# One order of the six matmuls of a tile in all plain products of a hybrid convolution encoder step

## The chip, the cores and the metric

The kernel runs as one program on one core of a Trainium2 chip. The metric is the device time of one execution in microseconds, taken as the median of three runs. The profile is of one more execution, whose own time is a little longer.

## What is computed

One layer of a streaming encoder for 576 tokens (512 of a new stream, 64 of a running one) with 1024 features: a SwiGLU feed-forward layer (FFN), a mixer with two gated convolution branches, a second FFN, and a final norm. Cut to the matrix products:

```python
def swiglu_ffn(x, w_gate_up, w_down):
    gate, up = jnp.split(x @ w_gate_up, 2, axis=-1)
    return (jax.nn.silu(gate) * up) @ w_down

def encoder_layer(...):
    x = x + 0.5 * swiglu_ffn(rms_norm(x, ffn1_norm), ffn1_w_gate_up, ffn1_w_down)
    h = rms_norm(x, mix_norm)
    p = h @ w_in          # 7 blocks of 1024: B, C, V of branch A; U (two) of branch B; two gates
    ...
    y_a = (a_b * a_conv) @ w_a_out
    ...
    y_b = b_act @ w_b_out
    merged = jax.nn.sigmoid(gate_a) * y_a + jax.nn.sigmoid(gate_b) * y_b
    x = x + merged @ w_out
    x = x + 0.5 * swiglu_ffn(rms_norm(x, ffn2_norm), ffn2_w_gate_up, ffn2_w_down)
```

Everything is float32.

## The kernel before

Features lie on the 128 partitions and the 576 tokens along the free axis, in two halves of 288 (`HALVES`, called half 0 and half 1 here). A product makes 128 output features for all tokens. It has one PSUM tile of two banks, one bank for each half, and adds up its input features in tiles of 128 (8 tiles for 1024 inputs, 5 or 6 for a group of hidden features of the FFN).

Each float32 operand is split into a high part, rounded to the format that TensorE takes at full rate (`float32r`), and the low rest. A tile of a product is then six matmuls of 128x128 weights against 128x288 activations: high weights by high activations, high weights by low activations, low weights by high activations, each for half 0 and half 1. In the code these are numbered `n` = 0, 1, 2 and `s` = 0, 1. Below they are written H0 and H1 (both high), L0 and L1 (low activations), W0 and W1 (low weights). All six add into the bank of their half, so any order gives the same sum up to rounding. Each matmul has its own weight load, also where two in a row use the same weights.

The order of the six is what the change is about. Before, there are six of them:

- `mm`, the ordinary one: H0 H1 L0 L1 W0 W1. It is used by the plain gate and up products of the FFNs, by the down projections ("d") and by `o`, the product with `w_out`.
- `THREES`, H0 L0 W0 H1 L1 W1: blocks 4 and 3 of `w_in` (branch B), 16 products.
- `MIRROR`, H0 L0 L1 H1 W1 W0: blocks 1, 2 and 0 (branch A), 24 products.
- `ALONE`, all eight tiles of half 0 (H0 L0 W0 each), then all eight of half 1: block 5 and `ya`, 16 products.
- `SIXES`, as ALONE but two tiles at a time: block 6, 8 products.
- `TWOS`, H0 L0 H1 L1 W0 W1: `yb`, 8 products.

In the order of time the program has: the start and three plain pairs of gate and up products; the other pairs of the first FFN, which are not plain (`pair` makes a gate and an up tile of seven half-size products, each with its own loop over H, L, W, untouched by the change); after each of four groups of hidden features, eight down projections; the mixer in the order of the list above from THREES to TWOS, then `o`; the second FFN with one plain pair; and a tail in which the last six down projections are done for 304 tokens and then for 272 (`LATE_SPANS`), with one span at a time.

Weights come by DMA from the SP queue; ScalarE (ACT) makes the high part, GpSimd (POOL) adds the low part up by a DMA. `ws.get` and `chunks` hand them over and issue the work for later ones. A product with a pattern or an order takes all its weights first and then issues its matmuls (`chunks`); an ordinary one takes them unit by unit (four tiles) in between. VectorE (DVE) reads the sums out of PSUM, and has the 31-tap convolution of branch B to do beside it: `fill` hands it pieces of that work by an estimate of how far it is behind TensorE, and the block of statements around `advance` makes the two sums of its layer norm on TensorE.

The instructions of each engine stand in the order in which the program is written.

Of the kernel before, what the change touches and what calls it, by code (L numbers as in the profile page):

```python
# [15 lines left out]
KT = D // P  # L16
# [6 lines left out]
H = T // 2  # L23
# [29 lines left out]
IN_TURN = (0, 4, 1, 5, 2, 6, 3, 7)  # L53


THREES = [(0, n, s) for s in range(2) for n in range(3)]
MIRROR = [(0, 0, 0), (0, 1, 0), (0, 1, 1), (0, 0, 1), (0, 2, 1), (0, 2, 0)]
TWOS = [(0, 0, 0), (0, 1, 0), (0, 0, 1), (0, 1, 1), (0, 2, 0), (0, 2, 1)]
SIXES = [(k, n, s) for s in range(2) for k in range(2) for n in range(3)]
ALONE = [(k, n, s) for s in range(2) for k in range(KT) for n in range(3)]  # L60

RAWS = 6

# [44 lines left out]
def tile_encoder_step(  # L108
# [7 lines left out]
    pe, dve, sca, pool = (  # L116
        Ordered(tc, e, c)
        for e, c in (
            (nc.tensor, pe_cost), (nc.vector, dve_cost), (nc.scalar, None), (nc.gpsimd, None)
        )  # L120
    )
# [31 lines left out]
    def psum2():  # L153
        return mmps.tile([P, 2, 512], F32, tag="mm", name=nm("mm"))
# [13 lines left out]
    def half(ap, s):  # L168
        return ap[:, s * H : (s + 1) * H]
# [223 lines left out]
    def mm(ps, w, kk, xs, first, last, spans=HALVES):  # L393


        (whi, wlo), (xh, xl) = w, xs
        for n, (a, b) in enumerate(((whi, xh), (whi, xl), (wlo, xh))):
            for s, (i, e) in enumerate(spans):
                pe.matmul(
                    ps[:, s, : e - i], a[:, kk, :], b[:, i:e],  # L400
                    start=first and n == 0, stop=last and n == 2,
                )

    def chunks(name):

        got = []
        for n in plan[name]:
            w = ws.get(n)
            got += [(w, kk) for kk in range(ws.units[n][1])]
        return got  # L410
# [10 lines left out]
    def take():  # L421

        while behind:
            ready, then = behind.pop(0)
            dve.time = max(dve.time, ready)
            then()

    early = {}

    def patterned(ps, got, xs, order, pattern):  # L430

        tiles = 1 + max(k for k, _, _ in pattern)
        todo = [
            (order[at + k], n, s) for at in range(0, len(xs), tiles) for k, n, s in pattern
        ]
        ends = {s: i for i, (_, _, s) in enumerate(todo)}
        begun = set()
        for i, (k, n, s) in enumerate(todo):
            ((whi, wlo), kk), (xh, xl) = got[k], xs[k]
            a, b = ((whi, xh), (whi, xl), (wlo, xh))[n]  # L440
            pe.matmul(
                ps[:, s, :H], a[:, kk, :], half(b, s), start=s not in begun, stop=ends[s] == i
            )
            begun.add(s)

    def product(name, xs, then=None, order=None, got=None, pattern=None):

        if name in early:
            return early.pop(name)[:, :, :H]
        ps = psum2()  # L450
        if pattern:
            patterned(ps, chunks(name), xs, order or range(len(xs)), pattern)
        elif order or got:
            got = got or chunks(name)
            for n, k in enumerate(order or range(len(xs))):
                mm(ps, *got[k], xs[k], n == 0, n == len(xs) - 1)
        else:
            k = 0
            for n in plan[name]:
                w = ws.get(n)  # L460
                for kk in range(ws.units[n][1]):
                    mm(ps, w, kk, xs[k], k == 0, k == len(xs) - 1)
                    k += 1
        take()
        if then is None:
            dve.time = max(dve.time, pe.time)
            return ps[:, :, :H]
        fill()
        behind.append((pe.time, lambda: then(ps[:, :, :H])))
# [145 lines left out]
    xg = []  # L615
# [58 lines left out]
    for k in range(KT):  # L674
        if k == KT - 1:
            R1 = rstd(ss)
        for name in FIRST:
            w, kk = firstw[name][k]
            mm(first[name], w, kk, xg[k], k == 0, k == KT - 1)
    early.update(first)  # L680
    name = ("f1", "u", 1)
    ps = product(name, xg)
# [131 lines left out]
    ss, xg = nss, nxg  # L814
# [71 lines left out]
    def gate_b(j, raw):  # L886
        def then(ps):
            t = gates[j] = ttile()
            if raw:
                dve.tensor_tensor(halves(t), ps, halves(R), op=ALU.mult)  # L890
                sca.activation(t, t, AF.Sigmoid)
                dve.tensor_tensor(t, t, R, op=ALU.mult)
            else:
                sca.activation(halves(t), ps, AF.Sigmoid)
        return then

    def value_b(j):
        G = gtile()
        history(G, HB, j, R_HB)

        def then(ps):
            gate(ps, gates.pop(j), G, HB)
            keep_history(G, HB, LB, j, 0)
            taps_of(j, G)
        return then

    for j in range(KT):
        raw = j < RAW_J
        xs = xg if raw else xn
        product(("p", 4, j), xs, gate_b(j, raw), pattern=THREES)  # L910
        if R is None:
            R = rstd(ss)
        if raw:
            xn.extend(scaled(range(3 * j, min(KT, 3 * j + 3)), R))
        product(("p", 3, j), xs, value_b(j), pattern=THREES)
    xg = xn

    AB = []
# [34 lines left out]

    for j in range(KT):
        for b, of in ((1, c_of), (2, cv_of), (0, b_of)):
            product(("p", b, j), xg, of(j), pattern=MIRROR)

    M, SGB, BA = [], [], []

# [23 lines left out]
    def ga_of(j):  # L983
        def then(ps):
            t = gates[j] = ttile()
            sca.activation(halves(t), ps, AF.Sigmoid)
        return then

    def ya_of(j):
        def then(ps):  # L990
            m = atile() if j < 4 else wtile(n=T)
            dve.tensor_tensor(halves(m), ps, halves(gates.pop(j)), op=ALU.mult)
            M.append(m)
        return then
# [22 lines left out]
    for j in range(KT):  # L1017
        if j == 5:
            while len(C) < KT:
                work.pop(0)()  # L1020
        product(("p", 5, j), xg, ga_of(j), pattern=ALONE)
        advance()
        product(("ya", j), AB, ya_of(j), pattern=ALONE)
        advance()
    take()
    sca.dma_start(hist.rearrange("(j p) n -> p j n", p=P), hst)
# [6 lines left out]
    def gb_of(j):  # L1033
        def then(ps):
            while work and j >= 2 and len(BA) < j - 1:
                work.pop(0)()
            sg = wtile(n=T) if j < 2 else gtile(n=T)
            sca.activation(halves(sg), ps, AF.Sigmoid)
            SGB.append(sg)
        return then  # L1040

    for j in range(KT):
        product(("p", 6, j), xg, gb_of(j), pattern=SIXES)
    while work:
        work.pop(0)()
    take()

    MS = []
    for j in range(KT):
        ps = product(("yb", j), BA, pattern=TWOS)  # L1050
        dve.tensor_tensor(halves(SGB[j]), ps, halves(SGB[j]), op=ALU.mult)
        dve.tensor_tensor(M[j], M[j], SGB[j], op=ALU.add)
        MS.append(split(M[j]))

    ss = Sum()
    xg = [None] * KT
    forms = Forms(R_N2)
    for n, j in enumerate(IN_TURN):
        ps = product(("o", j), MS)
# [4 lines left out]
        p = n // 2  # L1064
# [116 lines left out]
```

## Time and profile before

| what | value |
|---|---|
| median of 3 runs | 1329.13 us (1328.92 to 1329.64) |
| the profiled execution | 1331.87 us |
| its span, first to last instruction | 1330.1 us |
| TensorE busy, share of the span | 1301.9 us, 98% |
| matmul instructions | 9746 |
| VectorE, ScalarE, GpSimd busy | 895.4, 776.7, 399.8 us |
| mean granted TensorE clock | 0.996 of full speed |

A matmul's busy time in the trace is about 295 ns, but matmuls are pipelined and their records overlap, so the busy time says only that TensorE always had one in flight. What counts is the distance from the start of one matmul to the start of the next. The timeline gives it: it merges matmuls with operands of the same names into one row with a count, and since the weights of a product lie by turns in buffers `u`, `g` and `act`, a row is half a product (12, 18 or 24 matmuls). The start of a row less the start of an earlier one, over the matmuls in between, is the mean distance, called the pitch here.

### The profile page before, as it was taken

To read this page: it belongs to the slowest core of one execution; us is meant where nothing else is said; L and a number is where in the kernel's file an instruction comes from. 1 tells how busy PE (TensorE), PEld (TensorE's weight loads), DVE (VectorE), ACT (ScalarE), POOL (GpSimd) and SP (SyncE) were. 2 spreads that over 40 slices of the span, in tenths; PEclk is the share of its full clock that TensorE was granted. 3 is DMA by queue.
4 is the path that set the end of the run, shared out by engine and by line. 5 is a ranking of instruction groups with operands and counts; after the bars stand their busy time and mean duration, and the time that the engine had idled before them with its cause. 6 is when DMAs were issued, how large, how long until landed. Compare 5 with 4: busy or idle time off the path is not lost.

```text
span 1330.1 us, 25704 instructions
## 1 busy us (share of the span) xinstructions
PE 1301.9 (98%) x9746; PEld 1296.1 (97%) x9746; DVE 895.4 (67%) x1468; ACT 776.7 (58%) x1369; POOL 399.8 (30%) x504
## 2 busy tenths in 40 slices
PE   8999999999999999999999999999899999999995
PEld 8999999999999999999999999999899999999995
DVE  6848758748845998888884160336767858837944
ACT  8655646645666655555545574466665656644673
POOL 4142332232233453332222322221242242231242
PEclk9999999999999999999999999999999999999998
DMA  9497786886798897787775977775697696796692
GB/s 243 103 185 154 161 178 154 175 181 152 155 194 173 173 198 169 160 172 165 163 158 120 199 162 158 168 149 125 136 175 166 148 194 152 160 206 142 153 176 77
DMA packets 289564, 217.22 MB, mean 163 GB/s; under 512 B 15648, under 2 KB 251168, under 8 KB 289440
## 3 DMA queue, kind: packets, MB, share of 16 engines
q0 software_dynamic: 60192, 99.12, 45.4%
q1 hardware_dynamic: 227504, 115.62, 30.6%
q8 instruction: 77, 1.26, 0.4%
q10 hardware_dynamic: 1744, 0.84, 0.2%
q14 instruction: 47, 0.39, 0.1%
HBM read 113.81 MB, written 2.62 MB: 88 GB/s over the span
## 4 chain that ended last, share of the span: by engine, by line
PE 82%; issue 8%; DMA 3%; ACT 2%; DVE 2%; POOL 1%; DVEq 0%; SPq 0%; POOLq 0%; ACTq 0%
PE mm L84 82%; DMA g<-raw 1%; ACT g L84 1%; DVE tmp L84 1%; DMA raw<-in_ffn_w_gate_up_dram 1%; DMA raw<-in_ffn_w_down_dram 1%; DVE acc L84 1%; DMA act<-raw 1%; ACT tmp L84 1%; POOL g L84 0%; ACT u L84 0%; ACT act L84 0%; DVE g L84 0%; POOL act L84 0%; POOL u L84 0%
## 5 line engine op out<-in xcount | busy, mean ns | idle before, releaser
L84 PE MATMUL mm<-act,u 128*128 128x288 f32 x4668 | 668.2, 295 | 1.5 <-DMA u<-raw 1.5
L84 PEld LDWEIGHTS mm<-act,u 128*128 128x128 f32 x4668 | 636.1, 188 | 2.1 <-DMA u<-raw 1.8
L84 PE MATMUL mm<-act,g 128*128 128x288 f32 x2748 | 398.1, 295 | 6.6 <-DMA g<-raw 4.1
L84 PEld LDWEIGHTS mm<-act,g 128*128 128x128 f32 x2748 | 375.7, 188 | 8.0 <-DMA g<-raw 5.0
L84 POOL DMA_DIRECT2D u<-raw x203 | 176.6, 870 | 573.9 <-ACT u L84 520.4
L84 PE MATMUL mm<-act,act 128*128 128x288 f32 (+2 forms) x2280 | 321.0, 295 | 2.6 <-DVE act L84 1.3
L84 PEld LDWEIGHTS mm<-act,act 128*128 128x128 f32 x2280 | 308.4, 188 | 4.3 <-DVE act L84 2.3
L84 ACT CAST u<-raw 128x512 fp32r<-128x512 f32 (+2 forms) x203 | 116.5, 574 | 118.7 <-PE mm L84 93.0
L84 POOL DMA_DIRECT2D g<-raw x123 | 107.6, 875 | 255.9 <-ACT g L84 208.4
L84 DVE SCALAR_TENSOR_TENSOR w<-g,prm,w 128x606 f32<-128x606 f32 x232 | 179.4, 846 | 1.4 <-ACT w L84 1.4
L84 DVE TENSOR_TENSOR tmp<-mm,tmp 128x288 f32<-128x288 f32 (+1 forms) x244 | 110.0, 459 | 73.2 <-PE mm L84 56.0
L84 ACT ACTIVATE u<-u 128x512 fp32r<-128x512 f32 (+2 forms) x203 | 120.6, 594 | 6.4
L84 POOL DMA_DIRECT2D act<-raw x92 | 80.2, 872 | 50.6 <-ACT act L84 48.2
L84 DVE SCALAR_TENSOR_TENSOR tmp<-mm,r 128x576 f32<-128x576 f32 x48 | 36.3, 757 | 80.8 <-PE mm L84 80.7
L84 ACT CAST g<-raw 128x512 fp32r<-128x512 f32 (+2 forms) x123 | 67.3, 547 | 39.4 <-DMA raw<-in_ffn_w_down_dram 14.4
L84 ACT CAST act<-tmp 128x576 fp32r<-128x576 f32 x84 | 56.3, 674 | 55.1 <-DVE tmp L84 54.3
L84 ACT CAST g<-w 128x512 fp32r<-128x512 f32 x80 | 49.5, 619 | 66.5 <-DVE w L84 60.2
L84 ACT CAST u<-w 128x512 fp32r<-128x512 f32 x80 | 49.6, 620 | 64.4 <-DVE w L84 54.9
L84 DVE TENSOR_TENSOR act<-tmp,act 128x576 fp32r<-128x576 f32 x84 | 62.1, 754 | 19.9 <-ACT act L84 18.6
L84 ACT ACTIVATE g<-g 128x512 fp32r<-128x512 f32 (+2 forms) x123 | 69.9, 568 | 3.9
L84 ACT CAST act<-raw 128x512 fp32r<-128x512 f32 (+2 forms) x101 | 58.7, 581 | 17.7 <-PE mm L84 7.0
L84 DVE TENSOR_TENSOR w<-raw,raw 128x512 f32<-128x512 f32 x80 | 54.9, 686 | 9.3 <-DMA raw<-in_ffn_w_gate_up_dram 9.2
(87 smaller groups left out, 813.5 us busy)
## 6 DMA issues: line engine op xcount, KB each, us to landing
raw<-in_ffn_w_gate_up_dram SPq DMA_DIRECT2D x173, 256.0 KB, 3.4
u<-raw POOLq DMA_DIRECT2D x145, 256.0 KB, 3.9
raw<-in_w_in_dram SPq DMA_DIRECT2D x112, 256.0 KB, 3.1
act<-raw POOLq DMA_DIRECT2D x80, 256.0 KB, 4.3
raw<-in_ffn_w_down_dram SPq DMA_DIRECT2D x96, 192.0 KB, 3.4
g<-raw POOLq DMA_DIRECT2D x65, 256.0 KB, 3.7
g<-raw POOLq DMA_DIRECT2D x42, 192.0 KB, 4.4
u<-raw POOLq DMA_DIRECT2D x42, 192.0 KB, 4.3
```

Of the source, the lines that this page charges most:

```text
L84: return self.tc.keep_in_program_order(fn(*args, **kwargs))
```

## The change

The five patterns and `patterned` go. `mm`, and so every plain product, takes the six matmuls in one order, H0 L0 H1 L1 W0 W1, which is that of TWOS. In the tail, where there is one span, the rows with `s` = 1 are passed over and the order stays as it was. The half-size products of `pair` and the sums of the norms don't go through `mm`.

```diff
-THREES = [(0, n, s) for s in range(2) for n in range(3)]
-MIRROR = [(0, 0, 0), (0, 1, 0), (0, 1, 1), (0, 0, 1), (0, 2, 1), (0, 2, 0)]
-TWOS = [(0, 0, 0), (0, 1, 0), (0, 0, 1), (0, 1, 1), (0, 2, 0), (0, 2, 1)]
-SIXES = [(k, n, s) for s in range(2) for k in range(2) for n in range(3)]
-ALONE = [(k, n, s) for s in range(2) for k in range(KT) for n in range(3)]
+SIX = ((0, 0), (1, 0), (0, 1), (1, 1), (2, 0), (2, 1))
...
         (whi, wlo), (xh, xl) = w, xs
-        for n, (a, b) in enumerate(((whi, xh), (whi, xl), (wlo, xh))):
-            for s, (i, e) in enumerate(spans):
+        parts = ((whi, xh), (whi, xl), (wlo, xh))
+        for n, s in SIX:
+            if s < len(spans):
+                (a, b), (i, e) = parts[n], spans[s]
                 pe.matmul(
                     ps[:, s, : e - i], a[:, kk, :], b[:, i:e],
                     start=first and n == 0, stop=last and n == 2,
...
-    def product(name, xs, then=None, order=None, got=None, pattern=None):
+    def product(name, xs, then=None, order=None, got=None):
...
-        if pattern:
-            patterned(ps, chunks(name), xs, order or range(len(xs)), pattern)
-        elif order or got:
+        if order or got:
...
-        product(("p", 4, j), xs, gate_b(j, raw), pattern=THREES)
+        product(("p", 4, j), xs, gate_b(j, raw))
...
-        product(("p", 5, j), xg, ga_of(j), pattern=ALONE)
+        product(("p", 5, j), xg, ga_of(j))
...
-        ps = product(("yb", j), BA, pattern=TWOS)
+        ps = product(("yb", j), BA)
```

The other calls with a pattern change in the same way. On VectorE, ScalarE, GpSimd and SP the same instructions stand in the same order as before; only buffer numbers differ. What moves is on TensorE, and three places show it. In the rows the output stands before the arrow, then the activations, then the weights; two matmuls that differ only in the half of the tokens read alike and stand as one row with x2.

First, TensorE in a down projection of the first FFN, `mm_718`: its first two tiles before. `act_540` and `act_543` are the high and the low part of the activations, `u_694` and `u_695` those of the weights.

```order
L84 MATMUL mm_718_3707<-act_540_2764,u_694_3507 128x288 x2
L84 MATMUL mm_718_3707<-act_543_2782,u_694_3507 128x288 x2
L84 MATMUL mm_718_3707<-act_540_2764,u_695_3508 128x288 x2
L84 MATMUL mm_718_3707<-act_571_2917,u_694_3507 128x288 x2
L84 MATMUL mm_718_3707<-act_575_2936,u_694_3507 128x288 x2
L84 MATMUL mm_718_3707<-act_571_2917,u_695_3508 128x288 x2
```

And with the change, the first tile and the start of the second:

```order
L80 MATMUL mm_718_3707<-act_540_2764,u_694_3507 128x288
L80 MATMUL mm_718_3707<-act_543_2782,u_694_3507 128x288
L80 MATMUL mm_718_3707<-act_540_2764,u_694_3507 128x288
L80 MATMUL mm_718_3707<-act_543_2782,u_694_3507 128x288
L80 MATMUL mm_718_3707<-act_540_2764,u_695_3508 128x288 x2
L80 MATMUL mm_718_3707<-act_571_2917,u_694_3507 128x288
```

The matmul on the low activations now follows each one on the high activations within one half, where before the halves alternated.

Second, TensorE in a product of MIRROR, `mm_1228` (`act_1035` high, `act_1038` low activations; `u_1202` high, `u_1203` low weights), before:

```order
L84 MATMUL mm_1228_6951<-act_1035_5405,u_1202_6725 128x288
L84 MATMUL mm_1228_6951<-act_1038_5413,u_1202_6725 128x288 x2
L84 MATMUL mm_1228_6951<-act_1035_5405,u_1202_6725 128x288
L84 MATMUL mm_1228_6951<-act_1035_5405,u_1203_6726 128x288 x2
L84 MATMUL mm_1228_6951<-act_1036_5408,u_1202_6725 128x288
L84 MATMUL mm_1228_6951<-act_1039_5415,u_1202_6725 128x288 x2
```

And with the change:

```order
L80 MATMUL mm_1228_6951<-act_1035_5405,u_1202_6725 128x288
L80 MATMUL mm_1228_6951<-act_1038_5413,u_1202_6725 128x288
L80 MATMUL mm_1228_6951<-act_1035_5405,u_1202_6725 128x288
L80 MATMUL mm_1228_6951<-act_1038_5413,u_1202_6725 128x288
L80 MATMUL mm_1228_6951<-act_1035_5405,u_1203_6726 128x288 x2
L80 MATMUL mm_1228_6951<-act_1036_5408,u_1202_6725 128x288
```

Half 1 is now taken in the same sequence as half 0, high activations first.

Third, TensorE in a product of ALONE, `mm_1432` (`act_1217` high, `act_1218` low activations; `u_1405` high, `u_1406` low weights), before, where the first two tiles of half 0 follow each other:

```order
L84 MATMUL mm_1432_8628<-act_1217_6867,u_1405_8405 128x288
L84 MATMUL mm_1432_8628<-act_1218_6869,u_1405_8405 128x288
L84 MATMUL mm_1432_8628<-act_1217_6867,u_1406_8406 128x288
L84 MATMUL mm_1432_8628<-act_1244_7094,u_1405_8405 128x288
L84 MATMUL mm_1432_8628<-act_1245_7096,u_1405_8405 128x288
L84 MATMUL mm_1432_8628<-act_1244_7094,u_1406_8406 128x288
```

And with the change:

```order
L80 MATMUL mm_1432_8628<-act_1217_6867,u_1405_8405 128x288
L80 MATMUL mm_1432_8628<-act_1218_6869,u_1405_8405 128x288
L80 MATMUL mm_1432_8628<-act_1217_6867,u_1405_8405 128x288
L80 MATMUL mm_1432_8628<-act_1218_6869,u_1405_8405 128x288
L80 MATMUL mm_1432_8628<-act_1217_6867,u_1406_8406 128x288 x2
L80 MATMUL mm_1432_8628<-act_1244_7094,u_1405_8405 128x288
```

Both halves of a tile are now done before the next tile begins.

## Rows read from the trace of the kernel before

**Rows 1.** The page: span, busy time (share, count), granted clock in 40 slices.

```profile
span 1330.1 us, 25704 instructions
...
PE 1301.9 (98%) x9746; PEld 1296.1 (97%) x9746; DVE 895.4 (67%) x1468; ACT 776.7 (58%) x1369; POOL 399.8 (30%) x504
...
PEclk9999999999999999999999999999999999999998
```

**Rows 2.** The chain that ended last: start us, us, what.

```profile
76.47 641.55 PE mm L84 x4822
...
727.77 172.40 PE mm L84 x1299
...
958.37 270.81 PE mm L84 x2038
```

**Rows 3.** PE timeline: start us, us, instructions; down projections of the first FFN.

```profile
271.14 2.56 PE L84 MATMUL mm<-act,u 128*128 128x288 f32 x18
...
297.54 2.57 PE L84 MATMUL mm<-act,g 128*128 128x288 f32 x18
```

**Rows 4.** PE timeline, products in order THREES.

```profile
418.50 3.36 PE L84 MATMUL mm<-act,u 128*128 128x288 f32 x24
...
504.90 3.36 PE L84 MATMUL mm<-act,act 128*128 128x288 f32 x24
```

**Rows 5.** PE timeline, products in order MIRROR.

```profile
514.49 3.36 PE L84 MATMUL mm<-act,u 128*128 128x288 f32 x24
...
661.69 0.56 PE L84 MATMUL mm<-act,u 128*128 128x288 f32 x3
```

**Rows 6.** PE timeline, products in order ALONE.

```profile
668.05 1.75 PE L84 MATMUL mm<-act,u 128*128 128x288 f32 x12
...
671.21 1.76 PE L84 MATMUL mm<-act,u 128*128 128x288 f32 x12
...
674.41 1.74 PE L84 MATMUL mm<-act,u 128*128 128x288 f32 x12
...
706.21 0.69 PE L84 MATMUL mm<-tmp,ones_r 128*128 128x288 f32 x4
```

**Rows 7.** PE timeline, products in order SIXES.

```profile
772.83 3.35 PE L84 MATMUL mm<-act,u 128*128 128x288 f32 x24
...
817.44 0.43 PE L84 MATMUL mm<-act,u 128*128 128x288 f32 x2
```

**Rows 8.** PE timeline, products in order TWOS.

```profile
823.77 3.32 PE L84 MATMUL mm<-act,u 128*128 128x288 f32 x24
...
868.01 0.42 PE L84 MATMUL mm<-act,u 128*128 128x288 f32 x2
```

**Rows 9.** PE timeline, the products `o` in the order of `mm`.

```profile
874.39 3.36 PE L84 MATMUL mm<-act,u 128*128 128x288 f32 x24
...
919.20 0.42 PE L84 MATMUL mm<-act,u 128*128 128x288 f32 x2
```

**Rows 10.** PE timeline, gate and up products early in the first FFN.

```profile
36.79 3.28 PE L84 MATMUL mm<-act,g 128*128 128x288 f32 x24
...
49.27 0.42 PE L84 MATMUL mm<-act,g 128*128 128x288 f32 x2
```

**Rows 11.** Windows: A:B us, busy us (count) by engine, clock, DMA share, GB/s.

```profile
514.50:661.70 147.20, 147.20 (x1107) 147.20 (x1106) 123.92 (x195) 76.84 (x123) 43.72 (x77) 1.00 0.78 167
668.05:706.22 38.17, 38.17 (x291) 38.17 (x290) 28.40 (x40) 15.07 (x26) 10.35 (x12) 1.00 0.78 159
734.68:766.50 31.82, 31.82 (x243) 31.82 (x242) 2.42 (x4) 16.40 (x27) 9.31 (x12) 1.00 0.97 201
823.76:868.00 44.24, 44.24 (x338) 44.24 (x337) 15.93 (x21) 20.78 (x35) 12.04 (x14) 1.00 0.75 161
```

**Rows 12.** DVE timeline, the last step of the first normalisation sum.

```profile
698.91 0.76 DVE L84 TENSOR_TENSOR tmp<-acc,tmp 128x576 fp32r<-128x576 f32 x1 [0.74 <-ACT tmp L84]
```

**Rows 13.** PE timeline, the variance sum; idle before and its releaser in brackets.

```profile
726.98 0.40 PE L84 MATMUL mm<-tmp,ones_r 128*128 128x288 f32 x1 [1.02 <-ACT tmp L84]
```

More of the change, by code (lines that the diff above doesn't have):

```diff
@@ L428, in tile_encoder_step @@
     early = {}
[L430 to L444, printed above, removed]
-    def product(name, xs, then=None, order=None, got=None, pattern=None):
+    def product(name, xs, then=None, order=None, got=None):
         if name in early:
@@ L914, in tile_encoder_step @@
             xn.extend(scaled(range(3 * j, min(KT, 3 * j + 3)), R))
-        product(("p", 3, j), xs, value_b(j), pattern=THREES)
+        product(("p", 3, j), xs, value_b(j))
     xg = xn
@@ L955, in tile_encoder_step @@
         for b, of in ((1, c_of), (2, cv_of), (0, b_of)):
-            product(("p", b, j), xg, of(j), pattern=MIRROR)
+            product(("p", b, j), xg, of(j))
     M, SGB, BA = [], [], []
@@ L1020, in tile_encoder_step @@
                 work.pop(0)()
-        product(("p", 5, j), xg, ga_of(j), pattern=ALONE)
+        product(("p", 5, j), xg, ga_of(j))
         advance()
-        product(("ya", j), AB, ya_of(j), pattern=ALONE)
+        product(("ya", j), AB, ya_of(j))
         advance()
@@ L1042, in tile_encoder_step @@
     for j in range(KT):
-        product(("p", 6, j), xg, gb_of(j), pattern=SIXES)
+        product(("p", 6, j), xg, gb_of(j))
     while work:
```

## The prediction

> **What bounds the kernel now.** I read the page first. TensorE has a matmul in flight for 1301.9 of the 1330.1 us, 28.2 us less than the span, and its clock is granted in full in every slice but the last, so the level is 2.4 GHz nearly throughout [rows 1]. VectorE, with 895.4 us, is the next. The chain that ended last says where TensorE alone sets the time: from 76.47 us for 641.55 us, from 727.77 us for 172.40 us, and from 958.37 us for 270.81 us, 1084.8 us in all [rows 2]. Between these stretches, in the start and in the tail, other engines and DMAs have their turn. So a matmul made shorter inside the three stretches shortens the program, and one made shorter outside mostly lengthens a wait.
>
> The busy times say nothing of how long a matmul takes, since the records overlap. The timeline does, by the pitch. The reader is to see that the pitch isn't the same for all orders, although every matmul in these rows has 288 columns and full clock:
>
> - order of `mm`, down projections: (297.54 - 271.14) us over 11 rows of 18 matmuls = 26.40/198 = 133.3 ns [rows 3]; products `o`: 44.81/336 = 133.4 ns (14 rows of 24) [rows 9];
> - THREES: 86.40/648 = 133.3 ns (27 rows of 24) [rows 4];
> - MIRROR: 147.20/1104 = 133.3 ns (46 rows of 24) [rows 5];
> - ALONE: 38.16/288 = 132.5 ns (24 rows of 12) [rows 6]. Within a product the 24 matmuls of half 0 take 3.16 us (131.7 ns each) and those of half 1 3.20 us (133.3 ns);
> - SIXES: 44.61/336 = 132.8 ns (14 rows of 24) [rows 7];
> - TWOS: 44.24/336 = 131.7 ns (14 rows of 24) [rows 8].
>
> There is one exception. Three plain products early in the first FFN, in the order of `mm`, run at 130.0 ns (12.48/96, 4 rows of 24) [rows 10]. The same order thus has two steady pitches, and which of them it falls into isn't set by the order alone.
>
> **What the change does, part by part.** It adds no instruction and takes none away. On the engines beside TensorE nothing moves, so their work is costed at nothing, and no new wait is written. What remains is the pitch of each product that changes its order. I take TWOS for the new order's pitch, since it is the same sequence with the same shapes, and its 7 products in [rows 8] don't differ from each other. Against 131.67 ns a matmul gains 1.67 ns in the order of `mm`, THREES and MIRROR, 0.83 ns in ALONE and 1.10 ns in SIXES.
>
> By the stretches of the chain:
>
> - First stretch, down projections of the first FFN: 22 hidden tiles x 8 products x 6 = 1056 matmuls x 1.67 ns = 1.76 us. (They begin 2 us ahead of the stretch; that is 16 matmuls and left in.)
> - THREES, 16 products x 48 = 768 x 1.67 ns = 1.28 us.
> - MIRROR, 24 x 48 = 1152 x 1.67 ns = 1.92 us.
> - ALONE, 7 products before the mean of the layer norm at 706.21 us: 336 x 0.83 ns = 0.28 us.
> - ALONE, the 3 products between the mean and the variance: nothing. TensorE has the mean out by 706.21 us plus half a microsecond, then VectorE and ScalarE work on the variance, and TensorE waits for them for 1.02 us at 726.98 us [rows 6, 13]. What it gains here (144 x 0.83 ns = 0.12 us) it waits longer.
> - Second stretch: ALONE 6 products, 288 x 0.83 ns = 0.24 us; SIXES 384 x 1.10 ns = 0.42 us; TWOS nothing; `o` up to 900.2 us, 5 products, 240 x 1.67 ns = 0.40 us.
> - The other 3 products `o` (144 matmuls, 0.24 us) and the plain pair of the second FFN lie between the stretches. There the chain runs through the norm and the preparation of weights, and I count nothing.
> - Third stretch, down projections of the second FFN, three groups (16 hidden tiles x 8 x 6 = 768) x 1.67 ns = 1.28 us. The two products of the last group that change lie behind the stretch: nothing.
> - The start (FIRST and three more plain products, 288 matmuls): nothing, as the chain gets to TensorE alone only at 76.47 us. If the 130.0 ns of [rows 10] become 131.67 ns, 144 matmuls lose 0.24 us in a place where others are waited for.
>
> Sum: 1.76 + 1.28 + 1.92 + 0.28 + 0.24 + 0.42 + 0.40 + 1.28 = 7.58 us, so 7.6 us. The profiled execution took 1331.87 us, which becomes 1324.3 us. The median of the runs is 2.7 us below it, at 1329.13 us, and becomes 1321.5 us.
>
> **What could eat it.** The mixer's cover is VectorE: from 514.50 to 661.70 us it is busy for 123.92 of 147.20 us [rows 11]. TensorE comes out of the mixer 5.2 us earlier (the first four terms). The layer norm's first sum is ready on VectorE at 698.91 + 0.76 = 699.7 us, and TensorE takes it up at 706.21 us [rows 6, 12]. This is 6.5 us of room, more than the 5.2 us even if VectorE's work didn't move at all. So no new wait here; if the room were gone, each further microsecond of gain would be lost one for one.
>
> The bounds of the new pitch are the rows of 288 columns: 133.4 ns above (order of `mm`, [rows 9]) and 130.0 ns below [rows 10]. At the upper one the order of `mm`, THREES and MIRROR gain nothing, ALONE and SIXES lose 624 x 0.83 + 384 x 0.56 ns = 0.7 us and TWOS loses 384 x 1.67 ns = 0.6 us: 1330.5 us. At the lower one everything in the stretches, TWOS included, gains 1.67 ns more on 4992 + 384 = 5376 matmuls: 9.0 us further, 1312.5 us, of which the room of 6.5 us above would take back some.
>
> **The rivals.**
>
> *The pitch belongs to the stage, not to the order.* Each order but that of `mm` stands in one stage alone, so the table above could be one of stages: how much VectorE loads the memory, or where the buffers lie. For it: TWOS runs while VectorE is busy for 15.93 of 44.24 us, MIRROR while it is busy for 84% [rows 11]. Against it: ALONE has the same pitch with VectorE busy for 28.40 of 38.17 us and for 2.42 of 31.82 us (288 and 240 matmuls, 132.5 and 132.6 ns) [rows 11]; its two halves differ by 1.6 ns in alternating 3 us, in one stage and on the same weights [rows 6]; and `o`, with buffers like those of `yb` and next to it in time, goes back to 133.4 ns [rows 9]. In this case nothing changes: 1329.1 us. The Trainium skill speaks for this rival: "TensorE: Matmul & The Clock Gate", section "Back-to-back issue gap", gives the gap of an isolated matmul as columns over 2.4 GHz and 2.5 ns, from which 122.5 ns is my estimate for 288 columns, and makes it depend on the columns and the weight load, not on an order; by it the change is worth nothing. The trace differs from it, with 130.0 to 133.4 ns and a dependence on what follows what.
>
> *The new order has a second pitch too.* As that of `mm` has 130.0 and 133.3 ns [rows 3, 10], the new one may fall to 133.3 ns in some stages, most likely in the FFNs, where the down projections begin anew after half-size products four times each. Without these terms (1.76 + 1.28 us) the time is 1324.5 us. The other way, with 130.0 ns in the down projections, 1824 x 1.67 = 3.0 us more are gained: 1318.5 us.
>
> *Slower.* Two matmuls in a row now add into the same bank while VectorE and ScalarE read other banks, in the loaded stages as well. If the pair costs there, on the mean of the six, more than 133.4 + 2660/5000 = 133.9 ns, with 2660 ns being 0.2% and some 5000 matmuls that count, the kernel gets slower; at 135 ns it is 5000 x 1.6 ns = 8.0 us, 1337 us. Against it: THREES and MIRROR hold such pairs in loaded stages and don't go over 133.3 ns [rows 4, 5].
>
> **How the numbers follow.** The forecast, 131.7 ns everywhere, has 0.68. The rival of the stage has 0.10, the new order at 133.3 ns in the FFNs alone 0.09, at a lower pitch in places 0.09, slower 0.04. The predicted time is 1321.5 us; its own spread, by the terms counted at nothing (0.24 + 0.12 us one way, 0.3 us the other) and the run to run spread of 0.7 us, is about 1320.3 to 1322.7 us. The range takes in both sides of the second rival: 1318.0 to 1326.5 us, and leaves out the stage and slower, 0.14, with some of the lower pitch. A measurement tells 0.2% from no change, 2.7 us. Faster by more: 0.68 + 0.09 + 0.09 = 0.86; within: 0.10; slower: 0.04.
>
> **What would show it.** In the profile after, rows of 24 matmuls of THREES', MIRROR's and ALONE's products should lie 3.16 us apart instead of 3.20 and 3.18, and rows of 18 in the down projections 2.37 us instead of 2.40. The mean of the layer norm should come some 5.2 us earlier, and the wait at the variance be a tenth of a microsecond longer. The prediction is wrong if the rows stay at 3.20 us in a stage (then the stage, or a second pitch, decides), or if they shrink and the span doesn't: then waits behind 706 us or ahead of 958 us have grown, and the chain shows on whom.

## The result and the profile after

| what | before | after |
|---|---|---|
| median of 6 runs each, side by side | 1329.52 us (1328.92 to 1335.19) | 1321.66 us (1317.97 to 1325.34) |
| ratio, 95% interval | | 0.9933 (0.991 to 0.9957) |
| the profiled execution, its span | 1331.87, 1330.1 us | 1321.72, 1319.9 us |

The change made the kernel 7.9 us faster, by the medians. One thing stands out beside the median: the six runs after lie 7.4 us apart. The six before lie 6.3 us apart, but through one run at 1335.19 us alone; the other five lie within 0.9 us.

The page of the changed kernel: span and busy time. They answer to [rows 1].

```profile
span 1319.9 us, 25704 instructions
...
PE 1292.0 (98%) x9746; PEld 1286.4 (97%) x9746; DVE 895.2 (68%) x1468; ACT 776.6 (59%) x1369; POOL 400.9 (30%) x504
```

TensorE has the same 9746 matmuls, and the span is 10.2 us shorter. Of the chain that ended last in the changed kernel, two of the stretches in which TensorE alone sets the time (start us, us, what), which answer to [rows 2]:

```profile
719.12 172.87 PE mm L80 x1299
...
949.57 269.54 PE mm L80 x2038
```

The PE timeline of the changed kernel (start us, us, instructions; idle before and its releaser in brackets). In order: down projections of the first FFN (from 270.15 us), blocks 4 and 3 (from 416.74), blocks 1, 2 and 0 and the first product of block 5 (from 504.10), the time around mean and variance (from 697.55), block 6 (from 765.41), `yb` (from 809.65), `o` (from 860.21), down projections of the second FFN (from 1080.20).

```profile
270.15 2.53 PE L80 MATMUL mm<-act,u 128*128 128x288 f32 x18
...
296.22 2.53 PE L80 MATMUL mm<-act,g 128*128 128x288 f32 x18
...
416.74 3.28 PE L80 MATMUL mm<-act,u 128*128 128x288 f32 x24
...
504.10 3.28 PE L80 MATMUL mm<-act,u 128*128 128x288 f32 x24
...
660.10 3.28 PE L80 MATMUL mm<-act,u 128*128 128x288 f32 x24
...
697.55 0.69 PE L80 MATMUL mm<-tmp,ones_r 128*128 128x288 f32 x4
698.08 3.32 PE L80 MATMUL mm<-act,u 128*128 128x288 f32 x24
...
713.88 3.33 PE L80 MATMUL mm<-act,act 128*128 128x288 f32 x24
718.32 0.40 PE L80 MATMUL mm<-tmp,ones_r 128*128 128x288 f32 x1 [1.12 <-ACT tmp L80]
719.12 0.74 PE L80 MATMUL mm<-tmp,ones_r 128*128 128x288 f32 x3 [0.39 <-DVE tmp L80]
719.65 4.83 PE L80 MATMUL mm<-act,u 128*128 128x288 f32 x24
724.33 3.32 PE L80 MATMUL mm<-act,act 128*128 128x288 f32 x24
...
765.41 3.32 PE L80 MATMUL mm<-act,u 128*128 128x288 f32 x24
...
809.65 3.32 PE L80 MATMUL mm<-act,u 128*128 128x288 f32 x24
...
860.21 3.32 PE L80 MATMUL mm<-act,u 128*128 128x288 f32 x24
...
907.61 3.32 PE L80 MATMUL mm<-act,act 128*128 128x288 f32 x24
...
1080.20 2.53 PE L80 MATMUL mm<-act,g 128*128 128x288 f32 x18
...
1088.10 2.53 PE L80 MATMUL mm<-act,g 128*128 128x288 f32 x18
```

Worked out as ahead of the prediction, start less start over the matmuls in between:

- down projections of the first FFN, 26.07 us/198 = 131.7 ns (133.3 in [rows 3]);
- blocks 4 and 3, 87.36/672 = **130.0 ns** (133.3 in [rows 4]); blocks 1, 2 and 0 and a product of block 5, 156.00/1200 = **130.0 ns** (133.3 in [rows 5]);
- behind the mean 15.80/120 = 131.7 ns; block 6, 44.24/336 = 131.7 ns (132.8 in [rows 7]); `yb`, 50.56/384 = 131.7 ns as in [rows 8]; `o`, 47.40/360 = 131.7 ns (133.4 in [rows 9]); down projections of the second FFN, 7.90/60 = 131.7 ns.

So one order has two pitches within one execution. It goes from 131.7 to 130.0 ns at the sum of the norm ahead of 410.5 us and back at the mean at 697.55 us. Then there is the row at 719.65 us: 24 matmuls take 4.68 us to the next row, 1.5 us more than the 3.16 us of the others. The windows of the changed kernel (A:B, us, PE busy, granted clock, DMA share, GB/s) say why:

```profile
720.00:722.00 2.00, 2.00 (x10) 0.50 0.47 81
722.00:724.00 2.00, 2.00 (x14) 0.76 1.02 165
```

The granted clock is at its lower level of 1.2 GHz here, right behind the wait at the variance (1.12 and 0.39 us idle), and full again from 724 us. In [rows 13] the wait was nearly as long (1.02 us) and the clock stayed full.

### The profile page after: what moved, and what is told of

It is laid out like the page before. It is cut to its first block, busy times and chain, and to the rows that moved or that the text cites. A ratio compares the mean times of both kernels' runs of the same rounds, so it can differ in the third digit from the quotient of the medians.

```text
span 1319.9 us, 25704 instructions
## 1 busy us (share of the span) xinstructions
PE 1292.0 (98%) x9746; PEld 1286.4 (97%) x9746; DVE 895.2 (68%) x1468; ACT 776.6 (59%) x1369; POOL 400.9 (30%) x504
## 4 chain that ended last, share of the span: by engine, by line
PE 71%; issue 12%; DMA 6%; DVE 4%; ACT 4%; POOL 2%; POOLq 0%; DVEq 0%; SPq 0%; ACTq 0%
PE mm L80 71%; DMA u<-raw 2%; DVE tmp L80 1%; DMA raw<-in_ffn_w_gate_up_dram 1%; DMA raw<-in_ffn_w_down_dram 1%; DMA g<-raw 1%; ACT g L80 1%; ACT tmp L80 1%; ACT act L80 1%; ACT u L80 1%; POOL g L80 1%; DVE acc L80 1%; DVE w L80 1%; DVE g L80 1%; DMA act<-raw 1%
## 5 line engine op out<-in xcount | busy, mean ns | idle before, releaser
L80 PE MATMUL mm<-act,u 128*128 128x288 f32 x4668 | 661.1, 294 | 1.7 <-DMA u<-raw 1.5
L80 PE MATMUL mm<-act,act 128*128 128x288 f32 (+2 forms) x2280 | 314.0, 294 | 2.6 <-DVE act L80 1.6
L80 PEld LDWEIGHTS mm<-act,act 128*128 128x128 f32 x2280 | 303.7, 188 | 4.0 <-DVE act L80 2.3
```

The lines of the kernel that those rows point to most:

```text
L80: return self.tc.keep_in_program_order(fn(*args, **kwargs))
```

## The experiments

All are compared with runs of the kernel before on the same chip. Each kernel left one profile, so its pitches are those of one execution. The "theory of states" of the expectations is this: an order of the six matmuls doesn't have a pitch, it has a few steady ones; what interrupts the stream (a sum of a norm, a wait) puts TensorE into one of them, and it stays there until the next interruption, through other products and stages.

**again**: the changed kernel once more, unedited, for a second profile.

> The changed kernel itself, for a second profile and its spread. The theory: the new order has two steady pitches, 131.7 and 130.0 ns, and each execution falls into one of them where the chain of matmuls is broken (a wait, or the four matmuls of a norm's sum). In the first profile the mixer's first 46 products ran at 130.0 ns with a span of 1319.9 us. The theory expects executions from about 1316 to 1326 us, and a profile in which long pieces are at exactly 131.7 or exactly 130.0 ns; if the mixer is at 131.7 ns this time (2208 matmuls x 1.67 ns = 3.7 us), the span is about 1323 us. The rival, that the spread comes from DMAs or waits, expects the same pitch in each piece as before and idle time on TensorE that differs by microseconds.

Measured: 1324.58 us (8 runs, 1317.94 to 1327.21), ratio 0.9949 (0.9931 to 0.9967). Its PE timeline: blocks 4 and 3, the 3 products behind the mean, the last down projections of the first FFN, and the tail.

```profile
375.12 2.58 PE L80 MATMUL mm<-act,u 128*128 128x288 f32 x18
...
399.32 2.58 PE L80 MATMUL mm<-act,u 128*128 128x288 f32 x18
...
411.14 3.32 PE L80 MATMUL mm<-act,u 128*128 128x288 f32 x24
...
505.94 3.32 PE L80 MATMUL mm<-act,u 128*128 128x288 f32 x24
...
702.39 3.28 PE L80 MATMUL mm<-act,u 128*128 128x288 f32 x24
...
717.99 3.28 PE L80 MATMUL mm<-act,act 128*128 128x288 f32 x24
...
1281.79 3.06 PE L80 MATMUL mm<-act,act 128*128 128x304 f32 x18 [0.32 <-DMA act<-raw]
1285.18 2.81 PE L80 MATMUL mm<-act,act 128*128 128x304 f32 x18 [0.33 <-DMA act<-raw]
1288.92 3.30 PE L80 MATMUL mm<-act,act 128*128 128x304 f32 x22 [0.93 <-DMA act<-raw]
```

Its 8 runs lie 9.3 us apart, the 25 runs of the kernel before beside them 6.8 us.

Same program, other pitches: 94.80/720 = 131.7 ns in blocks 4 and 3, 15.60/120 = 130.0 ns behind the mean, and a third one, 24.20/180 = 134.4 ns, in the last group of down projections. So the pitch is no property of order and place. What an execution gains depends on which it falls into. This group shows it best: nine of the profiled kernels (all with the new order in `mm`) have the same instructions on TensorE up to here, and in it four of them run at 131.7 ns, three at 130.0 and two at 134.4.

**ffn_only, mixer_only, old_all**: parts of the change. The first has the new order in `mm` alone and keeps the patterns; the second keeps `mm` and replaces each pattern by TWOS; the third has one order everywhere, but that of `mm` before:

```diff
-SIX = ((0, 0), (1, 0), (0, 1), (1, 1), (2, 0), (2, 1))
+SIX = ((0, 0), (0, 1), (1, 0), (1, 1), (2, 0), (2, 1))
```

> The new order in the products of mm alone (down projections, the product with w_out, plain gate and up products); the mixer keeps its patterns. By the terms of the prediction (1.76 + 0.40 + 1.28 us) 3.4 us less than before, 1326.1 us, with a small spread, since THREES, MIRROR, ALONE and SIXES have shown one pitch each. The rival, that the stage sets the pitch and not the order, expects down projections at 133.3 ns and no gain.

> The new order in the mixer's patterned products alone, the products of mm in their old order. By the terms of the prediction (1.28 + 1.92 + 0.28 + 0.24 + 0.42 us) 4.1 us less than before, 1325.4 us, where the mixer is at 131.7 ns; where its first part is at 130.0 ns, up to 3.7 us less again, of which the wait at the variance may take some. Nearly all of the changed kernel's spread should be here. The rival of the stage expects 133.3 ns in the products of THREES and MIRROR.

> The changed kernel with the old order of mm (H0 H1 L0 L1 W0 W1) in all plain products, the mixer's too. The theory of the order: this order has the pitches 133.3 and 130.0 ns. At 133.3 ns throughout the mixer, ALONE's, SIXES' and TWOS' products lose 0.5 + 0.2 + 0.6 us: 1330.8 us. Where it falls to 130.0 ns in the mixer's first part, up to 7 us less, and a large spread. The rival of the stage expects the pitches of before in each stage, 132.5 ns in ALONE's and 131.7 ns in TWOS' products, and 1329.5 us.

Measured: `ffn_only` 1328.11 us, ratio 0.9982 (0.9973 to 0.999); `mixer_only` 1323.49 us, 0.9949 (0.9932 to 0.9966); `old_all` 1330.62 us, 1.0004 (0.9993 to 1.0014). So the order in the mixer alone gives most of the gain, though not all of it is had in the mixer, as its profile shows. And `old_all`, which takes the weights as the changed kernel does and gains nothing, shows that it is the order and not the end of the patterns. The sizes are off, to either side: 1.6 us for 3.4 and 6.3 us for 4.1. The profiles say how. The span of `ffn_only`, 1326.9 us, is 3.2 us below the profiled one of before, which fits, but the median of before lies below its own profile. And `mixer_only`, whose down projections in the second FFN keep the order of before, has them at 130.0 ns, which is 768 x 3.3 ns = 2.6 us of its 6.3 that no term foresaw. `old_all` falls on its expectation. Its PE timeline in `yb` and in the down projections of the second FFN:

```profile
821.88 3.36 PE L80 MATMUL mm<-act,act 128*128 128x288 f32 x24
...
860.27 3.36 PE L80 MATMUL mm<-act,act 128*128 128x288 f32 x24
...
1089.93 2.50 PE L80 MATMUL mm<-act,g 128*128 128x288 f32 x18
...
1097.73 2.50 PE L80 MATMUL mm<-act,g 128*128 128x288 f32 x18
```

`yb` goes from the 131.7 ns of [rows 8] to 38.39/288 = 133.3 ns with its order changed, and the stages of THREES and MIRROR have 133.3 ns in the old order and 131.7 or 130.0 ns in the two profiles of the new one, so the rival that the stage sets the pitch falls. But the old order, too, has more than one: 7.80/60 = 130.0 ns in the second FFN.

**before_again**: the kernel before, unedited.

> The kernel before, unchanged, for a second profile. Theory of states (each order has a few steady pitches, and an execution falls into one of them where the stream of matmuls is interrupted): the profiled execution before took 1331.87 us, 2 us more than the median of all later runs, so it is an unusual one; here the down projections of the second FFN should have 130.0 ns instead of 133.3 (768 x 3.33 ns = 2.6 us), the span being about 1327.5 us. Rival (the pitch of an order is fixed in each stage): 133.3 ns there again, span 1329 to 1330 us.

Measured: 1333.45 us, span 1331.7. The expectation failed. Its PE timeline in the same down projections:

```profile
1088.94 2.57 PE L84 MATMUL mm<-act,g 128*128 128x288 f32 x18
...
1096.94 2.57 PE L84 MATMUL mm<-act,g 128*128 128x288 f32 x18
```

8.00/60 = 133.3 ns, as in the first profile of before. But this program, too, changes its pitch from execution to execution: the plain products of [rows 10], at 130.0 ns there, run at 133.3 ns here (four rows from 37.08 to 49.88 us, 12.80/96). And what makes this execution the longer one lies in the tail. In the PE timeline of the first profile of before, and then of this one, the same 52 matmuls follow the wait for the last weights:

```profile
1294.48 7.34 PE L84 MATMUL mm<-act,act 128*128 128x304 f32 x52 [1.01 <-DMA act<-raw]
```

```profile
1294.68 8.79 PE L84 MATMUL mm<-act,act 128*128 128x304 f32 x52 [1.76 <-DMA act<-raw]
```

Here the granted clock is 0.50 from 1296 to 1298 us, behind the longer wait. That the ordinary runs of before, with medians of 1329.1 to 1329.7 us some 2.5 us below the first profile (1331.87), have 130.0 ns here (again 2.6 us) would fit, but no profile shows it.

**late_old**: the changed kernel with the old order in the down projections of the second FFN (groups one to three).

```diff
+        six = PAIRS if name[:2] == ("f2", "d") else SIX
```

> The changed kernel, with the down projections of the second FFN (groups one to three) back in the order H0 H1 L0 L1 W0 W1, in which two kernels of the first experiments ran them at 130.0 ns, against 131.67 ns in the new order. Theory of states: 130.0 ns in that stage, 768 x 1.67 ns = 1.3 us less than the changed kernel, ratio to the kernel before about 0.9938 (1321.5 us) where the copy of the changed kernel had 0.9949. Rival (133.3 ns is this order's own pitch, and the 130.0 ns belonged to those two kernels): 133.3 ns, 1.3 us more than the changed kernel, ratio 0.996 (1324 to 1326 us).

Measured: 1323.36 us (1319.64 to 1327.16), ratio 0.9947 (0.9927 to 0.9967). That whole stage has 130.0 ns, as the theory has it. The 1.3 us can't be told from the spread of the runs.

**shift**: the kernel before, with the activation buffers (`act`, and all that lies behind them, `g` too) 128 bytes further on; the `u` buffers stay.

```diff
+    gap = ctx.enter_context(tc.tile_pool(name="gap", bufs=1))
     act = ctx.enter_context(tc.tile_pool(name="act", bufs=44))
...
+    pool.memset(gap.tile([P, 32], F32, tag="gap", name="gap"), 0.0)
```

> The kernel before with all activation buffers moved up by 128 bytes, so that the offset of half 0 within 256 bytes becomes that of half 1 and the other way round. If the offset of a buffer sets the pitch, the two halves of the products in order ALONE change places (133.3 ns in half 0 and 131.7 in half 1 instead of 131.7 and 133.3), and other orders move too. Theory of states, order and interruption alone: 131.7 in half 0 and 133.3 ns in half 1 as before, THREES and MIRROR at 133.3 ns, and the down projections of the second FFN at 130.0 or 133.3 ns.

Measured: 1329.44 us in one run, beside a median of 1329.41 us. The halves of ALONE didn't change places, nor did they keep theirs: 132.5 and 132.6 ns in the mean of the 13 products that no wait follows, where the first profile of before has 131.7 and 133.4. The PE timeline of this kernel in `yb`:

```profile
822.22 3.36 PE L84 MATMUL mm<-act,u 128*128 128x288 f32 x24
825.42 3.28 PE L84 MATMUL mm<-act,act 128*128 128x288 f32 x24
828.54 3.36 PE L84 MATMUL mm<-act,u 128*128 128x288 f32 x24
```

Half products with weights in `u` take 3.20 us (133.3 ns), those with weights in `act` 3.12 us (130.0 ns), by turns, for the whole stage; in [rows 8] both took 3.16. Both expectations missed this: where the buffers lie also bears on the pitch. Whether it is the place of weights against activations, as the turns suggest, one profile can't show.

**breaks**: the changed kernel with extra matmuls ahead of each product of the mixer's first two stages, four each in blocks 4 and 3, one each in blocks 1, 2 and 0. They write into the bank that the product then starts anew.

```diff
         ps = psum2()
+        for n in range(BREAKS.get(name[:2], 0)):
+            pe.matmul(ps[:, n % 2, :H], ones_r, half(xs[0][0], n % 2), start=True, stop=True)
```

> The changed kernel with extra matmuls (ones as weights, 288 columns, their sum thrown away as the product starts anew in the same bank) ahead of each product of blocks 4 and 3 (four each) and of blocks 1, 2 and 0 (one each). Theory of states: each such interruption draws the pitch anew, so that products of both 131.67 and 130.0 ns follow each other within one stage, more than one change of pitch in 16 or 24 products, where the two profiles of the changed kernel had one pitch for a whole stage. If the interruption must be a wait and not merely other matmuls, all 16 and all 24 products keep one pitch. Extra time: 64 + 24 matmuls x 0.13 us = 11.5 us.

Measured: 1334.59 us. Its PE timeline where the fours end and the ones begin:

```profile
506.41 3.29 PE L82 MATMUL mm<-act,u 128*128 128x288 f32 x24
509.55 3.29 PE L82 MATMUL mm<-act,act 128*128 128x288 f32 x24
512.67 0.29 PE L82 MATMUL mm<-act,ones_r 128*128 128x288 f32 x1
512.80 3.39 PE L82 MATMUL mm<-act,u 128*128 128x288 f32 x24
516.02 3.39 PE L82 MATMUL mm<-act,act 128*128 128x288 f32 x24
```

The pitch isn't drawn anew at each place, as was expected; it follows the kind of interruption. Of the 15 products of blocks 4 and 3 behind the sum of the norm, the first has 131.7 ns and the other 14 have 130.0 ns but for a transition at their start (3.14 and 3.12 us a row here); with the first single one the row grows to 3.22 us, on the way to 134.4 ns, and all 24 products keep that. So do the next 6 products, which have no extra matmul, until the mean of the layer norm. The rival in that expectation, that it takes a wait, falls too.

**four_mix, two_mix, one_mix**: the ones that decide. The changed kernel with four, two or one extra matmul ahead of four products only, two early in the mixer and two behind the variance.

```diff
+EXTRA = 4
+PLACES = (("p", 3, 0), ("p", 4, 1), ("ya", 5), ("p", 5, 6))
...
+        for n in range(EXTRA if name in PLACES else 0):
+            pe.matmul(ps[:, n % 2, :H], ones_r, half(xs[0][0], n % 2), start=True, stop=True)
```

> The changed kernel with four extra matmuls (ones as weights, 288 columns, their sum thrown away) ahead of only four products: two early in the mixer and two behind the variance. Theory of states (what interrupts the stream chooses the pitch, which then holds until the next interruption): four extra matmuls led to 130.0 to 130.2 ns in 14 of 15 products of the earlier run, so most of the mixer and o should run at 130.0 ns; against 131.67 ns throughout that is 3800 x 1.67 = 6.3 us less, and the 16 extra matmuls cost 2.1 us: a span of about 1320 us, a ratio of 0.9915 to 0.993. Rival (the extra matmuls do nothing beyond their own time, and the 130.0 ns of that run came by chance): the pitches of the copy of the changed kernel, time 2.1 us above its 1324.6 us, ratio 0.9965.

> The same with one extra matmul at each of the four places. Theory of states: one extra matmul led to 134.4 ns in all 24 products of the earlier run, so four single matmuls, 0.5 us of work, should put the mixer up to the mean (2208 matmuls) and again the stretch behind the variance (some 1400) at 134.4 ns: 3600 x 2.77 ns = 10 us more than at 131.67 ns, the ratio near 1.000 to 1.003, as slow as the kernel before. Rival: 131.67 or 130.0 ns as in the changed kernel, 0.5 us more than its copy, ratio 0.995.

> The same with two extra matmuls at each of the four places, a number not tried so far. Theory of states: a steady pitch of 130.0, 131.67 or 134.4 ns behind the places, the same one in most executions, so that the runs spread less than those of the changed kernel (1318 to 1327 us). Rival (chance alone chooses the pitch): the same spread, median 1.1 us above the copy of the changed kernel, ratio 0.9957.

| extra matmuls at each place | median (runs) | lowest to highest | ratio (95%) |
|---|---|---|---|
| four | 1319.33 us (5) | 1318.23 to 1319.64 | 0.992 (0.9906 to 0.9933) |
| two | 1325.01 us (6) | 1323.16 to 1325.46 | 0.9961 (0.9948 to 0.9973) |
| one | 1331.25 us (12) | 1328.89 to 1335.98 | 1.0012 (1.0 to 1.0024) |

Adding 16 matmuls to 9746 gives the lowest median so far, adding 4 takes the whole gain of the change back. And with four the runs lie within 1.4 us and with two within 2.3, where the 14 runs of the changed kernel and its copy lie within 9.3; with one they lie 7.1 us apart. The PE timeline of the kernel with four, at the second place and 27 rows on:

```profile
412.70 3.33 PE L83 MATMUL mm<-act,act 128*128 128x288 f32 x24
415.87 0.70 PE L83 MATMUL mm<-act,ones_r 128*128 128x288 f32 x4
416.40 3.29 PE L83 MATMUL mm<-act,u 128*128 128x288 f32 x24
...
500.65 3.28 PE L83 MATMUL mm<-act,act 128*128 128x288 f32 x24
```

And of the kernel with one:

```profile
410.53 3.28 PE L83 MATMUL mm<-act,u 128*128 128x288 f32 x24
413.65 3.29 PE L83 MATMUL mm<-act,act 128*128 128x288 f32 x24
416.78 0.29 PE L83 MATMUL mm<-act,ones_r 128*128 128x288 f32 x1
416.91 3.39 PE L83 MATMUL mm<-act,u 128*128 128x288 f32 x24
...
500.80 3.39 PE L83 MATMUL mm<-act,u 128*128 128x288 f32 x24
```

At the same place and in the same stage: 84.25/648 = 130.0 ns and 83.89/624 = 134.4 ns. With two it is 131.7 ns in all 45 products up to the mean. Behind the variance, four gave 130.0 ns (at the second place) and two and one left 131.7 ns, so the kind of interruption isn't all: a single matmul gave 134.4 ns in the one place, not in the other. The expectation of 10 us for `one_mix` was too high by that.

The traces show what else counts: the pitch ahead of the interruption. The single matmul at 416.78 us came on a pitch of 130.0 ns (3.12 us from 410.53 to 413.65), those behind the variance on 131.7. All places in the profiles where products in the new order stand on both sides and TensorE doesn't wait, by the pitch behind:

| interruption | 130.0 ns ahead | 131.7 ns ahead | 134.4 ns ahead |
|---|---|---|---|
| the four matmuls of a norm's sum alone | 131.7 (7 of 7) | 130.0 (10 of 12), 131.7 (2) | 131.7 (4 of 4) |
| four extra | 130.0 (13 of 13) | 130.0 (6 of 7), 131.7 (1) | none |
| two extra | none | 131.7 (3 of 3) | none |
| one extra | 134.4 (2 of 2) | 131.7 (2 of 2) | 134.4 (23 of 23) |

So the pitch behind mostly follows from the kind of interruption and the pitch ahead, and what an execution falls into early reaches far. Four extra matmuls lead to 130.0 ns from either pitch but for one place, which fits the narrow runs of that kernel; one leads to 134.4 or 131.7 ns, which fits the wide ones. That the spread comes from this is argued, as the runs beside the profiled ones show no pitch.

**two_places**: the later place of each pair alone, four matmuls, with the second FFN as in `late_old`.

> A version that draws on what the earlier runs showed: the changed kernel with four extra matmuls at two places only (the later one of each pair of the earlier run, behind which its profile had 130.0 ns; the earlier one of each pair had left 131.67 ns), and with the down projections of the second FFN (groups one to three) in the order H0 H1 L0 L1 W0 W1. Theory of states: 130.0 ns behind both places and in the down projections of the second FFN; from 1319.3 us of the run with four places, less 8 extra matmuls (1.1 us) and 768 x 1.67 ns (1.3 us): 1317 us, a ratio of 0.990 to 0.991. Rival (it takes both interruptions of a pair, or the pitch was chance): 131.67 ns in the mixer, 1323 us or more, ratio 0.9955.

Measured: 1318.99 us (1317.66 to 1320.2), ratio 0.9923 (0.9909 to 0.9937). Behind each place the mixer has 130.0 ns as expected (the mean in between brings 131.7), and so have the down projections of the second FFN in the old order: one place of each pair does it. But the last down projections of the first FFN are at 134.4 ns here and were at 130.0 in `four_mix` (288 matmuls x 4.4 ns = 1.3 us), so the time isn't lower. The ratios of both kernels lie below the interval of the copy of the changed one (0.9949, from 0.9931), though the ends of the intervals still overlap a little. Against the first measurement of the change (0.9933, 0.991 to 0.9957) the intervals overlap, so that they beat it is likely, and not shown.

## Why the prediction was right, and where it wasn't

The median, the sign and the range held: 7.9 us of gain for 7.6. The picture behind the number held in parts, and a hit this close is in part luck: the eight runs of the changed kernel's copy gained 5.2 us, and the first profile came to its number by another way, as follows.

**The terms of the sum**, by the first matmul of each stage (start in us):

| stage | before | after | again |
|---|---|---|---|
| block 4 | 412.1 | 410.5 | 411.1 |
| block 1 | 508.1 | 504.1 | 505.9 |
| block 5 | 661.7 | 653.9 | 657.6 |
| mean | 706.2 | 697.6 | 701.9 |
| behind the variance | 728.3 | 719.7 | 724.0 |
| block 6 | 766.5 | 759.1 | 761.9 |
| `o` | 868.0 | 860.2 | 863.0 |
| plain pair, second FFN | 919.2 | 910.8 | 913.6 |
| d, second FFN | 982.0 | 973.3 | 976.0 |
| end of those | 1283.1 | 1272.9 | 1275.7 |
| last matmul | 1316.2 | 1306.0 | 1310.5 |

The lead over before grows in `again` from 1.0 to 2.2 us in blocks 4 and 3 (term 1.28), to 4.1 in blocks 1, 2, 0 (1.92), to 4.3 at the mean (0.28), by nothing up to the variance (0), by 0.24 to block 6 (0.24), by 0.4 in block 6 and nothing in `yb` (0.42, 0), by 0.6 in `o` (0.64 with the part counted at nothing), by 1.3 in the last stage (1.28). Wherever the pitch is 131.7 ns, the terms are right to 0.1 us. The first FFN left a lead of 1.0 us at block 4 in place of 1.76, since its last group fell to 134.4 ns.

**The step that failed** is "I take TWOS for the new order's pitch". The seven equal products of [rows 8] showed one pitch, and so it had 0.68, with 0.18 for a second pitch. [Rows 10] had already shown that one order can have two. Neither of the two profiles has 131.7 ns throughout. In the first, blocks 4 to 0 gained 6.2 us where the terms say 3.2 and ALONE 0.8 in place of 0.3, which is the rival of the lower pitch, in the mixer and not in the FFNs where I looked for it. So the pitch of one stage in one execution was no measure of the next.

**Terms at nothing weren't nothing.** The wait at the variance was to grow by 0.1 us, and did (1.02 to 1.12 us); but the lead shrank by 1.3 us between it and block 6, through the clock. And the tail took 1.7 us back in `again`: in the last three rows of its fence TensorE waits for weights that come by DMA, 0.32, 0.33 and 0.93 us, where the first profile of before has one such wait, of 1.01 us. I didn't try what makes them late. The other way, the lead grew by 0.5 us in `again` (0.4 in the first profile) between `o` and the last stage, where I counted nothing. In the first profile the extra 130.0 ns and these losses were of opposite sign.

**The step from profile to median** is open. I took the 2.7 us between the profiled execution before and the median as a fixed amount, and 0.7 us, from three runs, as the spread from run to run; 25 runs of before lie 6.8 us apart. Both profiles of before lie above the median of their neighbours (1331.87 and 1333.45 us against some 1329.5). Of the second, 2.3 us more than in the first lie in the tail, with its longer wait and its lower clock; what the ordinary runs do otherwise than the first isn't shown. From profile to profile the change gave 10.2 us, from median to median 7.9 and, for the copy, 5.2 us. All 14 runs of the two together have their median at 1322.8 us, and the slowest of them, 1327.21 us, is faster than the fastest of the 25 runs of before beside the copy, 1327.85 us.

**The room ahead of the mean** was there: VectorE's last step of the sum moved along. The DVE timeline of the changed kernel, which answers to [rows 12]:

```profile
690.60 0.76 DVE L80 TENSOR_TENSOR tmp<-acc,tmp 128x576 fp32r<-128x576 f32 x1 [0.74 <-ACT tmp L80]
```

It ends at 691.4 us and TensorE comes at 697.55, 6.2 us later (6.5 before), though it came 8.7 us earlier, more than the room.

**The rivals.** That the stage sets the pitch is refuted (`old_all`). That pairs in one bank cost: 134.4 ns, the pitch that this rival needs, does exist, in the last down projections of two kernels with the new order, and `one_mix`, at 1331.25 us, is about what the kernel would be if the first part of its mixer fell into it. So a pitch that makes the kernel slower is in reach, through another mechanism than the one I gave; none of the 14 unedited runs fell into it for that long, by their times. Of the Trainium skill ("TensorE: Matmul & The Clock Gate", "Back-to-back issue gap") no run here shows the gap, which the page gives for an isolated matmul: in these streams 130.0 ns was the least, against 122.5 ns as my estimate from it.

**What stays open**: what in TensorE holds a pitch, why an interruption and the pitch ahead of it lead into the one or the other, what sets the pitch of the early products, and why the clock fell behind the variance in this kernel.

## What to carry to other kernels

Before a pitch goes into a sum, look for a second one: in other stages with the same shapes, in a second profile, in the spread of the runs. A change to a long stream of equal matmuls can move it into another steady pitch for hundreds of microseconds, so a part of the gain belongs to the execution and not to the code; a few extra matmuls at a boundary are a cheap trial of whether a lower one is in reach. Where a kernel's runs spread far more than its neighbour's, compare the pitch by stage as well as the waits and the clock.

## What the runs showed of the hardware

- With 128x288 matmuls at full clock, the order H0 L0 H1 L1 W0 W1 runs at 130.0, 131.7 or 134.4 ns, and H0 H1 L0 L1 W0 W1 at 130.0 or 133.3 ns, each for long stretches and each in several profiles.
- One extra matmul took 45 products from 130.0 to 134.4 ns (`one_mix`), and left 131.7 ns as it was behind the variance; four took 131.7 to 130.0 ns (`four_mix`, `two_places`).
- With the activation buffers, and with them half of the weight buffers, moved by 128 bytes, the one profile taken has `yb` at 130.0 and 133.3 ns in turn, by weight buffer, in place of 131.7 ns.
- The granted clock fell to 0.50 behind 1.12 and 0.39 us of idle time at the variance, and cost 1.5 us. It fell there in the profiles of six kernels (after, `late_old`, `four_mix`, `two_mix`, `one_mix`, `two_places`), all with the new order in the whole mixer. The length of the wait doesn't tell these from the others: behind 1.38 us it fell in `late_old` and stayed full in `again`, behind 1.12 us it fell in the changed kernel and stayed full in `breaks`.
